# Whole loads of the branch inputs, eight sums moved to VectorE, and the second half of w_out loaded between evictions, in a hybrid pooling, convolution and attention block

## The chip, the cores and the metric

The kernel runs on one core of a Trainium2 chip. The metric is the device time of one execution in microseconds (us). Engines are named as in the profile: PE (TensorE, matrix products), PEld (its weight loads), DVE (VectorE), ACT (ScalarE), POOL (GpSimd), SP (SyncE, whose queue issues nearly all DMAs of this kernel).

## The reference

One layer over 1024 tokens of 1024 channels, in float32. A normed input is projected to ten groups of 512 columns and to 3 x 1024 merge-gate logits. Three branches (pooling, short convolution, stick-breaking attention) each give 512 channels, which are projected to 1024, weighted with a sigmoid gate and summed; an output projection and a norm follow.

```
def hybrid_layer(x, g_pre, w_in, pool_w, pool_scale, conv_w, conv_b, w_branch, w_out, g_post):
    h = rms_norm(x, g_pre)
    u = jnp.einsum('bsd,dn->bsn', h, w_in)
    (pool_v, pool_g, conv_x, conv_gb, conv_gc, conv_g,
     sb_q, sb_k, sb_v, sb_g, merge) = jnp.split(u, _split_points(), axis=-1)
    y_pool = pool_mixer(pool_v, pool_w, pool_scale) * jax.nn.silu(pool_g)
    y_conv = conv_mixer(conv_x, conv_gb, conv_gc, conv_w, conv_b) * jax.nn.silu(conv_g)
    y_sb = stick_breaking_attention(sb_q, sb_k, sb_v) * jax.nn.silu(sb_g)
    branches = jnp.stack([y_pool, y_conv, y_sb], axis=2)
    proj = jnp.einsum('bsnw,nwd->bsnd', branches, w_branch)
    gates = jax.nn.sigmoid(merge.reshape(b, s, N_BRANCH, D_MODEL))
    merged = jnp.sum(gates * proj, axis=2)
    out = jnp.einsum('bsd,de->bse', merged, w_out)
    return x + rms_norm(out, g_post)
```

## The kernel before

Activations lie with 128 channels on the partitions and the 1024 tokens along the free axis, in two halves of 512 (`HALVES`); blocks of 128 channels are numbered d = 0 to 7. Every product is made in three passes: both operands are split into a high and a low part (`split`: a cast to float32r on ACT for the high part, a subtraction on DVE or POOL for the low part), and low x high, high x low and high x high are accumulated in one PSUM bank of 128x512. So 12 products fill a bank of a half branch block, 24 one of the output projection.

The order of the work from the middle of the kernel on:

- **Gate pairs.** `gate_pair` makes two gate blocks of 128 channels from seven products of quarter blocks (`run_pair`, `product`). The products use three `g_ps` and two `q_ps` banks in turn. The results go into two tiles of tag `g` in the pool `gpool`, which has four such tiles of 128x1024; the pool also has two smaller tiles of tag `pr` (128x512).
- **First loop.** For the attention branch, four gate pairs multiply the projection that lies in DRAM (`proj_d`) by the gate and write it back (L695 to L700).
- **Pool branch.** `y_parts_of(yp_d)` loads the four blocks of the branch's output from DRAM in halves into the two `pr` tiles and splits them into `yhi` and `ylo` (pool `ypp`, four of each). `gated` then makes four pairs. After each pair, two branch blocks: `branch_proj` fills two `pp` banks of a pool of three (`ps_p`), 2 x 12 products, and `post` in `merged` multiplies by the gate (DVE, L716), adds the part so far, loaded from `proj_d` into `pr` tiles (POOL, L717), and writes the sum back (L722).
- **Conv branch.** The same with `y_parts_of(yc_d)`: two pairs with d = 0 to 3 in `gated`, then two pairs at once (`gs`, all four `g` tiles) and the **last four branch blocks**, d = 4 to 7, one after another. Their sums are not written back but split into the operands of the output projection (`take`, `take_merged`); `take` lags by one half. Meanwhile `taken_back` reads the sums of d = 0 to 3 back (`mr`) and splits them, and loads and splits the first half of w_out (`oh`).
- **Output projection.** The second half of w_out (`wo[1]`: load to one of three `wraw` tiles, cast on ACT, subtraction on POOL) is written in the code ahead of it. The tokens are worked in eight blocks of 128, first all with output columns 0 to 511, then all with 512 to 1023. Blocks 0 to 2 of the first half use the three `g` banks (`ahead`); from block 3 on `out_bank` alternates between `g` and `pp` banks. `first_half` squares a block's result with a row sum on ACT (L808) and scales it on DVE (L817), which frees the bank. In the second half the two variances are joined, and the result is scaled, added to x (`xr`, loaded into `g` tiles) and written out.

The order of the instructions on each engine is not that of the code alone: a planner arranges them when the program is built, by its own estimate of when each is ready, with earlier code first. On the chip every engine and SP's queue keep that order, and an instruction that waits holds what is behind it.

Of the kernel before, what the change touches and what calls it, by code (L numbers as in the profile page):

```python
# [8 lines left out]
F32 = mybir.dt.float32  # L9
F32R = mybir.dt.float32r  # L10
AF = mybir.ActivationFunctionType
ALU = mybir.AluOpType
PSUM = bass.MemoryType.PSUM

P = 128
D = 1024
S = 1024
KB = D // P
HALF = 512
# [7 lines left out]
HALVES = (slice(0, HALF), slice(HALF, S))  # L27
# [3 lines left out]
def f32(ap):  # L31
    return ap.bitcast(F32)
# [3 lines left out]
def hybrid_block_kernel(ctx, tc, x, g_pre, w_in, pool_w, pool_scale, conv_w, conv_b, w_branch, w_out, g_post, out):  # L36
# [12 lines left out]
    nc = tc.nc  # L49
    op = lambda name, bufs, **kw: ctx.enter_context(tc.tile_pool(name=name, bufs=bufs, **kw))  # L50

    const = op("const", 1)
    ps_g = op("ps_g", 3, space=PSUM)
# [18 lines left out]
    def split(raw, hi, lo, eng):  # L72
        nc.scalar.copy(hi, raw)  # L73
        eng.tensor_tensor(out=lo, in0=raw, in1=f32(hi), op=ALU.subtract)  # L74
# [29 lines left out]
    def next_w(ahead=2):  # L104
        while len(ready) < 1 + ahead:
            got = next(source, None)
            if got is None:
                break
            ready.append(got)
        return ready.pop(0)  # L110
# [210 lines left out]
    with tc.tile_pool(name="au", bufs=3) as au, \  # L321
# [106 lines left out]
        for n in range(len(steps) + LAG + 1):  # L428
            if n < len(steps):
                p, s, i = steps[n]  # L430
# [51 lines left out]
    def branch_proj(ys, weights, post, banks):  # L482
        whi, wlo = weights
        for t in range(2):
            pp = banks.tile([P, HALF], F32, tag="pp", name="pp")
            n = 0
            for k in range(NB):
                a = slice(k * P, (k + 1) * P)
                yh, yl = ys[k]
                for l, r in ((wlo, yh), (whi, yl), (whi, yh)):  # L490
                    nc.tensor.matmul(pp, l[:, a], r[:, HALVES[t]], start=(n == 0), stop=(n == 3 * NB - 1))  # L491
                    n += 1
            post(HALVES[t], pp)
# [49 lines left out]
    turn = [0]  # L543
# [133 lines left out]
    gpool = op("gates", 4, reuse_waits="tile")  # L677
# [6 lines left out]
    def part_of(src, ts):  # L684
        o = gpool.tile([P, HALF], F32, tag="pr", name="pr", bufs=2)
        nc.sync.dma_start(o, src[:, ts])
        return o

    def parts_in_dram(d):
        return [part_of(proj_d[d], ts) for ts in HALVES]  # L690
# [4 lines left out]
    for d in range(0, KB, 2):  # L695
        prs = parts_in_dram(d)
# [6 lines left out]
    def y_parts_of(srcs):  # L703
        parts = []
        for src in srcs:
            hi = ypp.tile([P, S], F32R, tag="yhi", name="yhi")
            lo = ypp.tile([P, S], F32R, tag="ylo", name="ylo")
            for ts in HALVES:
                split(part_of(src, ts), hi[:, ts], lo[:, ts], nc.vector)
            parts.append((hi, lo))  # L710
        return parts


    def merged(ys, d, g, prs, take):
        def post(ts, pp):
            nc.vector.tensor_tensor(out=g[:, ts], in0=pp, in1=g[:, ts], op=ALU.mult)  # L716
            nc.gpsimd.tensor_tensor(out=g[:, ts], in0=prs[0 if ts is HALVES[0] else 1], in1=g[:, ts], op=ALU.add)  # L717
            if take is not None:
                take(d, ts, g[:, ts])
        branch_proj(ys, next_w(), post, ps_p)  # L720
        if take is None:
            nc.sync.dma_start(proj_d[d], g)  # L722
# [16 lines left out]
    def out_weight(o, d, es):  # L739
        raw = wraw.tile([P, HALF], F32, tag="raw", name="wo_raw")  # L740
        nc.sync.dma_start(raw, w_out[d, :, es])
        split(raw, o[:, 0, :], o[:, 1, :], nc.gpsimd)
        return o[:, 0, :], o[:, 1, :]

    wo = ([], [])
# [16 lines left out]
    def take(*merged_half):  # L762

        waiting.append(merged_half)
        if len(waiting) > 1:
            take_merged(*waiting.pop(0))
        next(coming_back, None)

    gated(y_parts_of(yp_d))
    y_conv = y_parts_of(yc_d)  # L770
    gated(y_conv, 2)
    gs = gate_pair() + gate_pair()
# [10 lines left out]
    wo1p = op("wo1", KB, reuse_waits="tile")  # L783
    fin = held["m"]
    gpost_sb = fin.tile([P, D], F32, tag="gpost", name="gpost_sb")
    nc.sync.dma_start(gpost_sb, g_post.broadcast_to([P, D]))
    for d in range(KB):
        wo[1].append(out_weight(wo1p.tile([P, 2, HALF], F32R, tag="wo", name="wo"), d, HALVES[1]))


    def out_products(i, ps, ds, h, es):
        a = slice(i * P, (i + 1) * P)
        for d in ds:
            (mh, ml), (oh, ol) = m_parts[d], wo[h][d]
            for n, (l, r) in enumerate(((ml, oh), (mh, ol), (mh, oh))):
                nc.tensor.matmul(ps, l[:, a], r[:, es], start=(d == 0 and n == 0), stop=(d == KB - 1 and n == 2))  # L796

    turn = [0]

    def out_bank():  # L800
        turn[0] += 1
        return (ps_g.tile([P, HALF], F32, tag="g", name="o_ps") if turn[0] % 2
                else ps_p.tile([P, HALF], F32, tag="pp", name="o_ps"))

    def square(ps, var):
        junk = fin.tile([P, HALF], F32, tag="junk", name="junk")
        ssq = fin.tile([P, 1], F32, tag="ssq", name="ssq", bufs=4)
        nc.scalar.activation(junk[:, 0:ps.shape[-1]], ps, AF.Square, accum_out=ssq)  # L808
        o = fin.tile([P, 1], F32, tag="var", name="var", bufs=S // P + 4)
        if var is None:  # L810
            nc.vector.tensor_scalar(out=o, in0=ssq, scalar1=1.0 / D, scalar2=EPS, op0=ALU.mult, op1=ALU.add)
        else:
            nc.vector.scalar_tensor_tensor(out=o, in0=ssq, scalar=1.0 / D, in1=var, op0=ALU.mult, op1=ALU.add)
        return o

    def scaled(ps, o, es):
        nc.vector.tensor_tensor(out=o, in0=ps, in1=gpost_sb[:, es], op=ALU.mult)  # L817
# [3 lines left out]
    def first_half(i, ps):  # L821
        kept_var.append(square(ps, None))
        o = (held["raw"].tile([P, HALF], F32, tag="raw", name="o0") if i < 5
             else held["sum"].tile([P, HALF], F32, tag="s", name="o0"))
        scaled(ps, o, HALVES[0])
        kept_o.append(o)
# [6 lines left out]
    for i in range(n_tok):  # L833
        if i < 3:
            ps = ahead[i]
        else:
            ps = out_bank()
            out_products(i, ps, range(KB), 0, slice(0, HALF))
        first_half(i, ps)
    for i in range(n_tok):  # L840
        a = slice(i * P, (i + 1) * P)
        xr = gpool.tile([P, D], F32, tag="g", name="xr")
        nc.sync.dma_start(xr, x[a, :])
        o1 = gpool.tile([P, HALF], F32, tag="pr", name="o1", bufs=2)
        var = kept_var[i]
        pieces = (slice(0, HALF),) if i < n_tok - 1 else (slice(0, 256), slice(256, HALF))
        for es in pieces:
            ps = out_bank()[:, 0:es.stop - es.start]
            out_products(i, ps, range(KB), 1, es)
            var = square(ps, var)  # L850
            scaled(ps, o1[:, es], slice(HALF + es.start, HALF + es.stop))
        r = fin.tile([P, 1], F32, tag="rstd", name="rstd", bufs=2)
        nc.gpsimd.tensor_tensor(out=r, in0=var, in1=expo[:, 0:1], op=ALU.pow)
        for o, es in [(kept_o[i], HALVES[0])] + [(o1[:, es], slice(HALF + es.start, HALF + es.stop)) for es in pieces]:
            nc.vector.scalar_tensor_tensor(out=o, in0=o, scalar=r, in1=xr[:, es], op0=ALU.mult, op1=ALU.add)
            nc.sync.dma_start(out[a, es], o)
# [41 lines left out]
```

## Time and profile before

| | |
|---|---|
| median of 3 runs | 1049.41 us (1045.95 to 1049.87) |
| profiled execution | 1049.73 us, its span 1048.0 us |
| PE busy | 1004.6 us, 96% of the span |
| DVE, ACT, POOL busy | 625.9, 449.4, 460.1 us |
| mean granted TensorE clock | 0.988 |
| data moved | 97.09 MB, mean 93 GB/s |

The span is the time from the first to the last instruction on the core. In the list of waits a row reads: engine, tile and line of the instruction that waited, what it waited for, total, number of times, longest. In a timeline a row reads: start, length, engine, line, operation, output and inputs, count, and in brackets the engine's idle time before it with what ended it. A group's row gives the busy time and the mean of one in ns, then the idle time before them. For DMAs the time given is from the issue to the landing. A row of a tile gives minimum, median and maximum of an operation's length, and first and last start.

### The profile page before, as it was taken

The numbers are of one execution on the slowest core, as the hardware profiler recorded it, in microseconds if no ns is written. First come the engines' busy times: TensorE is split into PE (matmuls) and PEld (weight loads), VectorE is DVE, ScalarE is ACT, GpSimd is POOL, SyncE is SP. The second block draws the span as 40 slices with busy tenths as digits, with TensorE's granted clock in tenths as the row PEclk, the third lists the DMA queues.
The fourth block names the chain that finished last, engine by engine and source line by source line (L and its number), as shares of the span: only waits on it lengthen the run. The fifth ranks groups of instructions, "written<-read, shape, count | busy, mean of one in ns | idle before, by whom it ended". The sixth has DMA issues, their size and how long they took to land.

```text
span 1048.0 us, 13308 instructions
## 1 busy us (share of the span) xinstructions
PE 1004.6 (96%) x4752; PEld 829.0 (79%) x4752; DVE 625.9 (60%) x847; ACT 449.4 (43%) x879; POOL 460.1 (44%) x367
## 2 busy tenths in 40 slices
PE   4999999999998999999999999998999999998997
PEld 3788878888887888888888888886888888876886
DVE  6556777667777968798677675554333543342133
ACT  6567667567755543332222234333233332443111
POOL 3043544535472024455454444444555555576000
PEclk9999999999999999999999999998999999999999
DMA  6101000101011532122122134545333454164033
GB/s 229 53 21 41 22 21 21 41 21 32 21 31 41 191 131 71 61 70 91 61 81 61 61 111 144 190 136 173 118 120 124 161 171 131 34 221 157 1 121 121
DMA packets 45138, 97.09 MB, mean 93 GB/s; under 512 B 5392, under 2 KB 5648, under 8 KB 45072
## 3 DMA queue, kind: packets, MB, share of 16 engines
q1 hardware_dynamic: 44928, 95.71, 28.0%
q8 instruction: 38, 0.62, 0.2%
q10 hardware_dynamic: 144, 0.52, 0.1%
q14 instruction: 28, 0.23, 0.1%
HBM read 73.15 MB, written 23.07 MB: 92 GB/s over the span
## 4 chain that ended last, share of the span: by engine, by line
PE 82%; ACT 5%; DVE 4%; POOL 4%; issue 3%; DMA 2%; POOLq 0%; SPq 0%; DVEq 0%; ACTq 0%
PE g_ps L539 26%; PE q_ps L539 17%; PE g_ps L189 12%; PE pp L491 10%; PE o_ps L796 7%; PE o L418 3%; PE tp L404 2%; DVE sn L386 2%; PE z L382 1%; PE z L379 1%; ACT sn L383 1%; POOL sp L388 1%; POOL g L717 1%; DMA pr<-yp 1%; DMA xt<-in_x_dram 1%
## 5 line engine op out<-in xcount | busy, mean ns | idle before, releaser
L74 POOL TENSOR_TENSOR w_lo<-s,w_hi 128x512 fp32r<-128x512 f32 x95 | 130.7, 1376 | 173.8 <-ACT w_hi L73 171.2
L74 POOL TENSOR_TENSOR w_lo<-s_raw,w_hi 128x512 fp32r<-128x512 f32 x70 | 94.6, 1351 | 102.6 <-ACT w_hi L73 96.8
L388 POOL TENSOR_TENSOR sp<-sp,sn 128x127 f32<-128x127 f32 (+3 forms) x64 | 81.2, 1272 | 132.8 <-DVE sn L386 69.0
L386 DVE TENSOR_TENSOR_SCAN sn<-sn,zeros 128x128 f32<-128x128 f32 (+3 forms) x64 | 100.6, 1574 | 48.2 <-ACT sn L383 45.5
L73 ACT CAST w_hi<-s 128x512 fp32r<-128x512 f32 x96 | 59.6, 621 | 134.1 <-PE g_ps L539 65.7
L73 ACT CAST w_hi<-s_raw 128x512 fp32r<-128x512 f32 x70 | 43.5, 621 | 138.2 <-PE g_ps L539 53.8
L189 PE MATMUL g_ps<-hh,w_hi 128*128 128x512 f32 x240 | 99.4, 414 | 0.3 <-ACT hh L285 0.3
L189 PE MATMUL g_ps<-hl,w_hi 128*128 128x512 f32 x240 | 94.5, 394 | 0.3 <-DVE hl L286 0.3
L189 PE MATMUL g_ps<-hh,w_lo 128*128 128x512 f32 x240 | 94.5, 394 | 0.0
L74 POOL TENSOR_TENSOR w_lo<-w_raw,w_hi 128x512 fp32r<-128x512 f32 x44 | 68.2, 1550 | 56.3 <-ACT w_hi L73 56.3
L539 PE MATMUL g_ps<-hh,w_hi 128*128 128x512 f32 x236 | 92.6, 392 | 0.0
L539 PE MATMUL g_ps<-hh,w_lo 128*128 128x512 f32 x236 | 92.1, 390 | 0.0
L539 PE MATMUL g_ps<-hl,w_hi 128*128 128x512 f32 x236 | 91.8, 389 | 0.0
L491 PE MATMUL pp<-yhi,w_lo 128*128 128x512 f32 x192 | 77.1, 402 | 5.0 <-ACT yhi L73 2.6
L491 PE MATMUL pp<-ylo,w_hi 128*128 128x512 f32 x192 | 76.8, 401 | 0.9 <-DVE ylo L74 0.9
L491 PE MATMUL pp<-yhi,w_hi 128*128 128x512 f32 x192 | 76.4, 399 | 0.0
L383 ACT ACTIVATE sn<-z 128x384 f32<-128x384 f32 (+2 forms) x96 | 47.9, 499 | 29.7 <-PE z L382 20.3
L232 DVE TENSOR_TENSOR wl<-tp,wh 128x512 fp32r<-128x512 f32 (+2 forms) x96 | 50.4, 545 | 15.4 <-ACT wh L405 14.9
L539 PE MATMUL q_ps<-hh,w_hi 128*128 128x512 f32 x148 | 58.1, 392 | 0.0
L539 PE MATMUL q_ps<-hh,w_lo 128*128 128x512 f32 x148 | 57.8, 391 | 0.0
L539 PE MATMUL q_ps<-hl,w_hi 128*128 128x512 f32 x148 | 57.5, 389 | 0.0
L405 ACT CAST wh<-tp 128x512 fp32r<-128x512 f32 (+2 forms) x96 | 44.6, 493 | 21.8 <-PE tp L404 17.2
(204 smaller groups left out, 2426.4 us busy)
## 6 DMA issues: line engine op xcount, KB each, us to landing
s_raw<-in_w_in_dram SPq DMA_DIRECT2D x96, 256.0 KB, 2.6
pr<-proj SPq DMA_DIRECT2D x48, 256.0 KB, 3.3
proj<-g SPq DMA_DIRECT2D x20, 512.0 KB, 2.9
w_raw<-in_w_in_dram SPq DMA_DIRECT2D x34, 256.0 KB, 2.6
w_raw<-in_w_branch_dram SPq DMA_DIRECT2D x24, 256.0 KB, 2.6
xt<-in_x_dram SPq DMA_DIRECT2D x8, 512.0 KB, 7.9
proj<-proj SPq DMA_DIRECT2D x8, 512.0 KB, 2.7
wo_raw<-in_w_out_dram SPq DMA_DIRECT2D x16, 256.0 KB, 2.9
```

What stands on the lines that cost most here:

```text
L73: nc.scalar.copy(hi, raw)
L74: eng.tensor_tensor(out=lo, in0=raw, in1=f32(hi), op=ALU.subtract)
L189: nc.tensor.matmul(ps, l[:, a], r[k // 4][t][:, k % 4, :], start=(n == 0), stop=(n == 3 * KB - 1))
L232: nc.vector.tensor_tensor(out=o, in0=a, in1=f32(b), op=ALU.subtract)
L383: nc.scalar.activation(sn[:, c0:c1], z[:, :w], AF.Sigmoid, scale=-0.125)
L386: nc.vector.tensor_tensor_scan(out=rev, data0=rev, data1=zeros.to_broadcast([P, n]), initial=1.0, op0=ALU.mult, op1=ALU.max)
L388: nc.gpsimd.tensor_tensor(out=sp[:, 0:n - 1], in0=sp[:, 0:n - 1], in1=sn[:, 1:n], op=ALU.mult)
L405: nc.scalar.copy(wh[c][:, 0:m, qsub], tp[:, 0:m, :])
L418: nc.tensor.matmul(o[:, cs], vc[:, j, s, :], wt[j // 4][:, j % 4, cs], start=(j == 0 and wt is wl), stop=(j == i and wt is wh))
L491: nc.tensor.matmul(pp, l[:, a], r[:, HALVES[t]], start=(n == 0), stop=(n == 3 * NB - 1))
L539: nc.tensor.matmul(bank, l[:, a], r[:, j, :], start=(n == 0), stop=(n == 11))
L796: nc.tensor.matmul(ps, l[:, a], r[:, es], start=(d == 0 and n == 0), stop=(d == KB - 1 and n == 2))
```

## The change

Three edits. (1) `y_parts_of` loads each block of a branch's output whole, 128x1024 in one DMA, into a tile of tag `g`, and splits it with one cast and one subtraction; the `pr` tiles are no longer used for it. (2) In `merged`, where `take` is given (the last four branch blocks), the sum of L717 is made by DVE in place of POOL; elsewhere it stays on POOL. (3) The loads and splits of the second half of w_out move from ahead of the output projection into its first loop, one behind each `first_half`; and `out_bank` gives a `pp` bank for its first three calls (blocks 3, 4 and 5) and then a `g` bank on even turns, a `pp` bank on odd ones.

```
--- before.py
+++ after.py
@@ -705,8 +705,9 @@
         for src in srcs:
             hi = ypp.tile([P, S], F32R, tag="yhi", name="yhi")
             lo = ypp.tile([P, S], F32R, tag="ylo", name="ylo")
-            for ts in HALVES:
-                split(part_of(src, ts), hi[:, ts], lo[:, ts], nc.vector)
+            y = gpool.tile([P, S], F32, tag="g", name="y")
+            nc.sync.dma_start(y, src)
+            split(y, hi, lo, nc.vector)
             parts.append((hi, lo))
         return parts
 
@@ -714,7 +715,8 @@
     def merged(ys, d, g, prs, take):
         def post(ts, pp):
             nc.vector.tensor_tensor(out=g[:, ts], in0=pp, in1=g[:, ts], op=ALU.mult)
-            nc.gpsimd.tensor_tensor(out=g[:, ts], in0=prs[0 if ts is HALVES[0] else 1], in1=g[:, ts], op=ALU.add)
+            adder = nc.gpsimd if take is None else nc.vector
+            adder.tensor_tensor(out=g[:, ts], in0=prs[0 if ts is HALVES[0] else 1], in1=g[:, ts], op=ALU.add)
             if take is not None:
                 take(d, ts, g[:, ts])
         branch_proj(ys, next_w(), post, ps_p)
@@ -784,8 +786,6 @@
     fin = held["m"]
     gpost_sb = fin.tile([P, D], F32, tag="gpost", name="gpost_sb")
     nc.sync.dma_start(gpost_sb, g_post.broadcast_to([P, D]))
-    for d in range(KB):
-        wo[1].append(out_weight(wo1p.tile([P, 2, HALF], F32R, tag="wo", name="wo"), d, HALVES[1]))
 
 
     def out_products(i, ps, ds, h, es):
@@ -799,7 +799,7 @@
 
     def out_bank():
         turn[0] += 1
-        return (ps_g.tile([P, HALF], F32, tag="g", name="o_ps") if turn[0] % 2
+        return (ps_g.tile([P, HALF], F32, tag="g", name="o_ps") if turn[0] > 3 and turn[0] % 2 == 0
                 else ps_p.tile([P, HALF], F32, tag="pp", name="o_ps"))
 
     def square(ps, var):
@@ -837,6 +837,7 @@
             ps = out_bank()
             out_products(i, ps, range(KB), 0, slice(0, HALF))
         first_half(i, ps)
+        wo[1].append(out_weight(wo1p.tile([P, 2, HALF], F32R, tag="wo", name="wo"), i, HALVES[1]))
     for i in range(n_tok):
         a = slice(i * P, (i + 1) * P)
         xr = gpool.tile([P, D], F32, tag="g", name="xr")
```

More of the change, by code (lines that the diff above doesn't have):

```diff
@@ L707, in y_parts_of @@
             lo = ypp.tile([P, S], F32R, tag="ylo", name="ylo")
-            for ts in HALVES:
-                split(part_of(src, ts), hi[:, ts], lo[:, ts], nc.vector)
+            y = gpool.tile([P, S], F32, tag="g", name="y")
+            nc.sync.dma_start(y, src)
+            split(y, hi, lo, nc.vector)
             parts.append((hi, lo))
@@ L716, in post @@
             nc.vector.tensor_tensor(out=g[:, ts], in0=pp, in1=g[:, ts], op=ALU.mult)
-            nc.gpsimd.tensor_tensor(out=g[:, ts], in0=prs[0 if ts is HALVES[0] else 1], in1=g[:, ts], op=ALU.add)
+            adder = nc.gpsimd if take is None else nc.vector
+            adder.tensor_tensor(out=g[:, ts], in0=prs[0 if ts is HALVES[0] else 1], in1=g[:, ts], op=ALU.add)
             if take is not None:
@@ L786, in hybrid_block_kernel @@
     nc.sync.dma_start(gpost_sb, g_post.broadcast_to([P, D]))
-    for d in range(KB):
-        wo[1].append(out_weight(wo1p.tile([P, 2, HALF], F32R, tag="wo", name="wo"), d, HALVES[1]))
     def out_products(i, ps, ds, h, es):
@@ L801, in out_bank @@
         turn[0] += 1
-        return (ps_g.tile([P, HALF], F32, tag="g", name="o_ps") if turn[0] % 2
+        return (ps_g.tile([P, HALF], F32, tag="g", name="o_ps") if turn[0] > 3 and turn[0] % 2 == 0
                 else ps_p.tile([P, HALF], F32, tag="pp", name="o_ps"))
@@ L839, in hybrid_block_kernel @@
         first_half(i, ps)
+        wo[1].append(out_weight(wo1p.tile([P, 2, HALF], F32R, tag="wo", name="wo"), i, HALVES[1]))
     for i in range(n_tok):
```

## The prediction

> **What bounds the kernel.** I read the page's top first, then the list of TensorE's own waits, then windows over the stages of the change.
>
> ```profile
> span 1048.0 us, 13308 instructions
> PE 1004.6 (96%) x4752; PEld 829.0 (79%) x4752; DVE 625.9 (60%) x847; ACT 449.4 (43%) x879; POOL 460.1 (44%) x367
> ```
>
> TensorE is busy 96% of the span, and the change takes no product away. What it can win is idle TensorE time and time at a reduced clock, nothing else. So the list of waits comes next (total, times, longest); these four rows are the ones in the part that the change touches:
>
> ```profile
> PE o_ps L796 <- DVE o L817: 4.7, 1, 4.7
> PE pp L491 <- ACT yhi L73: 2.6, 2, 1.4
> PE pp L491 <- DVE g L716: 2.4, 2, 2.1
> PE pp L491 <- DVE ylo L74: 0.9, 1, 0.9
> ```
>
> Each edit has its wait: the staging of the pool branch's y (2.6 + 0.9), the last four branch blocks (2.4), the start of the output projection (4.7). A wait costs more than its own length, which the windows show; PEclk is the granted clock.
>
> ```profile
> core 0: us, PE busy (x) PEld busy (x) DVE busy (x) ACT busy (x) POOL busy (x), PEclk, DMA share, GB/s
> 711.72:729.54 17.82, 14.32 (x50) 10.53 (x49) 7.79 (x11) 5.82 (x10) 7.67 (x6) 0.81 0.50 170
> 749.06:759.94 10.88, 10.88 (x49) 9.01 (x49) 2.77 (x4) 1.74 (x3) 6.42 (x5) 1.00 0.35 117
> 919.48:945.82 26.34, 23.93 (x98) 19.03 (x96) 12.09 (x16) 10.76 (x18) 18.61 (x13) 0.94 0.67 221
> 945.82:1041.80 95.98, 91.07 (x409) 74.70 (x407) 25.88 (x52) 17.53 (x45) 20.38 (x20) 0.96 0.29 96
> ```
>
> The second row is the yardstick: two branch blocks (48 products) without a wait take 10.88. The first row is the same work behind the staging: 17.82 at a mean clock of 0.81, so **6.94 lost**, 3.5 by waiting and about 0.19 x 17.82 = 3.4 by the clock. The third holds the last four blocks: 26.34 against 2 x 10.88 = 21.76, **4.58 lost**, 2.4 by waiting and 0.06 x 26.34 = 1.6 by the clock. The fourth, the output projection, comes below.
>
> **Part by part. 1, whole loads into gate tiles (L705 to L709).** Now:
>
> ```profile
> 686.79 2.38 SPq L129 DMA_DIRECT2D s_raw<-in_w_in_dram  x2
> 687.63 0.68 DVE L585 TENSOR_TENSOR g<-q_ps,u 128x512 f32<-128x512 f32 x1
> 694.89 1.06 SPq L700 DMA_DIRECT2D proj<-g  x2
> 696.00 1.76 SPq L686 DMA_DIRECT2D pr<-yp  x2
> 697.80 7.94 SPq L129 DMA_DIRECT2D s_raw<-in_w_in_dram  x2
> 715.92 1.62 SPq L686 DMA_DIRECT2D pr<-yp  x2
> 702.86 0.62 ACT L73 CAST yhi<-pr 128x512 fp32r<-128x512 f32 x1 [4.39 <-DMA pr<-yp]
> proj<-g SPq DMA_DIRECT2D x20, 512.0 KB, 2.9
> mr<-proj SPq DMA_DIRECT2D x4, 512.0 KB, 4.7
> DMA to landing us min/median/max: 2.6/3.6/6.8
> L74 DVE TENSOR_TENSOR m<-mr,m 128x1024 fp32r<-128x1024 f32 x4 | 5.5, 1386 | 2.6 <-ACT m L73 2.6
> L73 ACT CAST m<-mr 128x1024 fp32r<-128x1024 f32 x4 | 4.2, 1046 | 0.6 <-DMA mr<-proj 0.6
> 885.22 0.32 SPq L722 DMA_DIRECT2D proj<-g  x1
> 936.37 0.38 SPq L843 DMA_DIRECT2D xr<-in_x_dram  x1
> ```
>
> Eight half loads go two by two through the two pr tiles, which the proj loads hold until 696; the last pair starts at 715.92, four microseconds after TensorE is ready for it (711.72). After the change four loads of 512 KB use the four gate tiles. Gate tiles seem to be handed out in the order of the code: one pair's write-back at 885.22 freed two, yet the later xr loads, which need only such a tile, begin at 936.37. So y0 and y1 wait until the pair before has its second tile, first written at 687.63, and then take the two tiles of the pair before that, long written back. Put behind the two s_raw loads that SP issues there (686.79 to 689.2), they start near 689 and land by 694 (4.7 for a 512 KB read), 2 us before the first half load is even issued now. y2 and y3 take the tiles whose write-back is issued at 694.89 (landing after 2.9) or those of y0 and y1 after their split: issued near 698.5, landed between 703 and, with the slowest landing of a yp load (6.8, the row of minimum, median and maximum), 706. One cast and one subtraction of 128x1024 each (1.05 and 1.39, the m<-mr rows) put the last operand at about 708.5. TensorE needs y0 at 711.7 and y3, its tenth to twelfth product there, 9 x 10.88 / 48 = 2.0 later, at 713.7. Slack: 5 us. In the worst placement, y2 and y3 stand on SP behind the s_raw pair that holds the queue from 697.80 for 7.94: issued at 705.8, landed at 710.5 to 712.6, ready at 713 to 715. That is a wait of 0 to 1.5; with a little more on DVE, 2. **Take -6.94**; bounds 0 (the loads are as late as now) and -6.94.
>
> The first gate tile of the next pair is handed out behind y3. It is wanted near 701 and a tile is free from about 698.5. Should it be late, TensorE still has the five banks that products use in turn. Eight DMA issues leave SP; DVE and ACT process the same elements in half as many instructions. The conv branch's y is staged the same way at 820 to 840, under a pair of gates, where the list shows no wait of TensorE before and I expect none after: 0. What is next in line behind the y parts is the first branch weight; its cast stands on ACT behind the y casts and comes forward with them.
>
> **2, sums by VectorE (L717).** Eight additions leave POOL for DVE.
>
> ```profile
> 937.22 0.68 DVE L716 TENSOR_TENSOR g<-pp,g 128x512 f32<-128x512 f32 x1
> 942.20 0.68 DVE L716 TENSOR_TENSOR g<-pp,g 128x512 f32<-128x512 f32 x1
> 934.64 1.29 POOL L717 TENSOR_TENSOR g<-pr,g 128x512 f32<-128x512 f32 x1
> 935.96 0.62 ACT L73 CAST m<-g 128x512 fp32r<-128x512 f32 x1 [4.04 <-POOL g L717]
> L717 POOL TENSOR_TENSOR g<-pr,g 128x512 f32<-128x512 f32 x8 | 10.3, 1286 | 4.1 <-DVE g L716 4.1
> L716 DVE TENSOR_TENSOR g<-pp,g 128x512 f32<-128x512 f32 x8 | 5.5, 684 | 0.8 <-PE pp L491 0.8
> L74 DVE TENSOR_TENSOR m<-g,m 128x512 fp32r<-128x512 f32 x8 | 6.4, 805 | 20.0 <-ACT m L73 20.0
> L699 DVE TENSOR_TENSOR g<-g,pr 128x512 f32<-128x512 f32 x16 | 14.4, 903 | 8.5 <-ACT g L594 8.4
> L133 DVE TENSOR_TENSOR s<-s_raw x14: 691/693/1776, 697.8 to 893.9; 128x512 f32<-128x512 f32 x14
> ```
>
> The chain of one half is product, DVE multiplication, POOL addition, ACT cast, DVE subtraction. The subtraction stands on DVE ahead of a later multiplication, so the multiplication, which frees the pp bank, waits for POOL: the fourth (937.22) and the fifth (942.20) lie 5.0 apart, where the list has TensorE wait for them. POOL has 10.3 of additions here between weight splits. On DVE one addition costs between 0.69 and 1.78 (the ends of L133, same shapes and also two SBUF inputs); I take 0.90, the mean of L699, which reads the same tiles. A half is then 0.68 + 0.90 + 0.81 = 2.39, under the 2.72 that TensorE takes for it (10.88 / 4). From the first multiplication near 922.2, with two of the four mr subtractions (2.8) still to do, the fifth starts by 922.2 + 4 x 2.39 + 2.8 = 934.6 and ends at 935.3. The eighth half, which needs that bank, starts at 919.48 + 7 x 2.72 = 938.5: 3.2 in hand. With 1.78 each it would be 0.3 late. The pr load of the half after next also starts earlier. **Take -4.58**; bounds -4.58 and 0.
>
> The Trainium skill, "SBUF — State Buffer", section "Who interferes with whom", speaks against this edit: a DVE instruction with two SBUF inputs and a GpSimd instruction reading SBUF exclude each other, the later one waiting the whole instruction. The L133 maximum agrees: 0.69 plus nearly a POOL operation of 1.29 is near 1.78. By it, if every addition met a POOL operation, the sum would lose the 0.3 above and no more.
>
> **3, second half of w_out and other banks (L787, L802).**
>
> ```profile
> 953.21 1.66 ACT L73 CAST wo<-wo_raw 128x512 fp32r<-128x512 f32 x3
> 964.92 1.32 ACT L73 CAST wo<-wo_raw 128x512 fp32r<-128x512 f32 x2 [1.29 <-DMA wo_raw<-in_w_out_dram]
> 966.14 0.59 ACT L808 ACTIVATE junk<-o_ps 128x512 f32<-128x512 f32 x1
> 980.76 0.60 ACT L808 ACTIVATE junk<-o_ps 128x512 f32<-128x512 f32 x1 [4.39 <-issue]
> 986.28 0.60 ACT L808 ACTIVATE junk<-o_ps 128x512 f32<-128x512 f32 x1 [4.83 <-issue]
> 997.07 44.48 PE L796 MATMUL o_ps<-wo,m 128*128 128x512 f32 x216
> ```
>
> Eight wo casts, 953.21 to 966.1, stand on ACT ahead of the first square (966.14), and token block 3 wants the bank that this square and its DVE partner free. Undisturbed, a token block takes 5.52 (986.28 - 980.76), so the first half is 8 x 5.52 = 44.16; the second takes 44.48; together 88.64. TensorE ran from 945.82 to 997.07 + 44.48 = 1041.55, 95.73: **7.09 lost**, 4.7 waiting and the rest clock. Afterwards blocks 3, 4 and 5 go to the three pp banks, free since the last branch block, so the first bank is wanted again after six blocks (33 us), not three. That alone covers the late square. The moved loads keep their eight DMAs on SP, eight casts and eight POOL splits. Even if ACT kept every wo behind its block's square, the last one, cast after block 7, is split 0.8 + 0.6 + 1.3 later, while its product is 21 products of 0.23 (5.52 / 24) = 4.8 into the second half; with its load (as long as one of 512 KB, 2.9) behind as well it would be 0.8 late, and such a gap could bring the half clock (1.6, as in the third window). **Take -7.09**; bounds -7.09 and -4.6.
>
> **Sum.** 1049.73 (the profiled execution; span 1048.0) - 6.94 - 4.58 - 7.09 = 1031.12. The median of the runs, 1049.41, is 0.3 lower, so the sum serves for both; I say 1031.
>
> **Rivals.** (a) The staging wait survives in part: the worst placement of part 1, 2 us of wait. The third window shows that one gap of 2.1 brought the half clock, so another 1.6 (its clock loss above) to 3.4: 1035 to 1036.5. For: SP is a single queue and was held 7.94 there. Against: 5 us of slack otherwise. The Trainium skill, "TensorE: Matmul & The Clock Gate", section "Why this matters for your kernels", advises only against gaps over about 3 us; by it this rival costs 2, but the 0.94 clock behind a 2.1 gap decides otherwise.
> (b) DVE becomes the limit of the last four blocks, by contention with POOL or an addition waiting for its pr load with the multiplication queued behind: up to all 4.58 back, 1035.7. For: DVE work is 2.39 of each 2.72. Against: three banks of lead.
> (c) Slower: the new loads and additions give another order on the engines in the seven gate pairs between 730 and 919, so that weights miss their product there. Place: each pair's first product; price: a wait of 2.1 and 1.6 of clock, 3.7 per pair as in the third window. Five pairs (18.5) eat the gain, and it is slower than before by more than a measurement tells from the seventh: 25.9 - 18.6 = 7.3 over, 1057. Against: TensorE has no wait there now, and those lines stay.
> (d) No change: the y loads get no tile before 698 and go two by two as now, and DVE is the limit too; only part 3 is left, and a block of weights late by 0.8 with two half-clock windows takes 3.4 of it: 1046.
>
> **How the numbers follow.** Forecast 0.70, (a) 0.12, (b) 0.10, (c) 0.03, (d) 0.05. A measurement of this kernel tells about 0.5% (5 us) from no change. Faster: forecast, (a) and (b), 0.92; same 0.05; slower 0.03. The range goes from 1027 (the lowest run before lay 3.5 under the median, so a run may come out that much lower) to 1038 (a or b, or a little of both).
>
> **What would show it.** Right: no TensorE wait on yhi, ylo, g L716 or o L817 in the list; 48 products after 711.7 in about 10.9; four last blocks in 21.8; output projection 88.6; clock 1.00 in all three; yp loads issued near 689 and 698. Wrong: a wait on yhi from a load after 705; DVE additions above 1.5 with a wait on g L716; squares or second-half products waiting on wo; any new wait between 730 and 919.

## The result, and the profile after

The changed kernel takes **1032.44 us** (median of 4 runs, 1032.07 to 1033.10) against 1048.99 us before (4 runs, 1045.95 to 1049.87), a ratio of **0.9837** (95% interval 0.9818 to 0.9856). The forecast was 1031, range 1027 to 1038. The profiled execution took 1032.51.

The top of the page after, and the whole list of TensorE's waits from 600 us on (total, times, longest). Lines from L709 on have moved by two at most: the multiplication of `merged` is now L717, its sum L719.

```profile
span 1030.7 us, 13275 instructions
PE 997.1 (97%) x4752; PEld 825.0 (80%) x4752; DVE 636.5 (62%) x847; ACT 447.8 (43%) x871; POOL 453.0 (44%) x359
```

```profile
PE pp L491 <- DVE g L717: 0.7, 1, 0.7
```

Of the four rows of before one is left, and it is short. The same stages as windows (columns as in the prediction; the granted clock is the third number from the end):

```profile
711.81:722.69 10.88, 10.88 (x49) 9.01 (x48) 2.97 (x5) 2.98 (x6) 7.67 (x6) 1.00 0.48 154
912.99:935.77 22.78, 22.10 (x97) 17.95 (x96) 19.09 (x22) 10.82 (x18) 12.93 (x8) 1.00 0.76 250
935.77:1024.41 88.64, 88.64 (x409) 73.16 (x407) 28.26 (x54) 17.33 (x43) 16.98 (x17) 1.00 0.31 105
```

The two blocks behind the staging take 10.88, the yardstick exactly: 6.94 won. The last four blocks take 22.78: 3.56 won, with 1.02 over the yardstick's 21.76. The output projection takes 88.64, the number worked out for it undisturbed: 7.09 won. The three make 17.59 (6.94 + 3.56 + 7.09); the two profiled executions differ by 17.22, and the 0.4 between these numbers is less than the 1.0 by which the runs after differ among themselves.

The timelines of the staging after, SP's queue, then rows of DVE and ACT, show how near the y parts came to their computed times:

```profile
687.32 0.90 SPq L709 DMA_DIRECT2D y<-yp  x2
693.52 2.71 SPq L709 DMA_DIRECT2D y<-yp  x2
696.51 2.02 SPq L700 DMA_DIRECT2D proj<-g  x2
692.27 1.23 DVE L74 TENSOR_TENSOR ylo<-y,yhi 128x1024 fp32r<-128x1024 f32 x1
694.66 1.23 DVE L74 TENSOR_TENSOR ylo<-y,yhi 128x1024 fp32r<-128x1024 f32 x1 [0.56 <-ACT yhi L73]
701.18 1.05 ACT L73 CAST yhi<-y 128x1024 fp32r<-128x1024 f32 x1 [2.04 <-DMA y<-yp]
702.87 2.34 DVE L74 TENSOR_TENSOR ylo<-y,yhi 128x1024 fp32r<-128x1024 f32 x1
```

Two loads go out at 687.3, about when the pair before first writes its second tile (687.79); the other two are issued from 693.52 on, right behind the end of y0's subtraction (692.27 + 1.23 = 693.50) and before the write-backs are issued (696.51), so they took the tiles of y0 and y1. Two gate tiles thus carried all four loads, where the prediction spoke of four. The last subtraction ends at 705.2, where 708.5 was forecast, 8.5 us before its first use.

### The profile page after: what moved, and what is told of

Same layout as the page of the kernel before. It is cut to its first block, busy times and chain, and to the rows that moved or that the text cites. A ratio compares the mean times of both kernels' runs of the same rounds, so it can differ in the third digit from the quotient of the medians.

```text
span 1030.7 us, 13275 instructions
## 1 busy us (share of the span) xinstructions
PE 997.1 (97%) x4752; PEld 825.0 (80%) x4752; DVE 636.5 (62%) x847; ACT 447.8 (43%) x871; POOL 453.0 (44%) x359
## 4 chain that ended last, share of the span: by engine, by line
PE 84%; ACT 5%; DVE 4%; POOL 3%; issue 2%; DMA 2%; SPq 0%; POOLq 0%; DVEq 0%; ACTq 0%
PE g_ps L539 26%; PE q_ps L539 17%; PE g_ps L189 12%; PE pp L491 11%; PE o_ps L796 8%; PE o L418 3%; PE tp L404 2%; DVE sn L386 2%; PE z L382 1%; PE z L379 1%; POOL w_lo L74 1%; POOL sp L388 1%; ACT sn L383 1%; DMA xt<-in_x_dram 1%; ACT sp L384 1%
## 5 line engine op out<-in xcount | busy, mean ns | idle before, releaser
L491 PE MATMUL pp<-yhi,w_lo 128*128 128x512 f32 x192 | 75.0, 392 | 0.7 <-DVE g L717 0.7
L383 ACT ACTIVATE sn<-z 128x384 f32<-128x384 f32 (+2 forms) x96 | 47.9, 499 | 29.7 <-PE z L382 20.4
L133 DVE TENSOR_TENSOR s<-s_raw 128x512 f32<-128x512 f32 x48 | 41.9, 873 | 23.4 <-POOL w_lo L74 22.8
```

What stands on the lines that cost most here:

```text
L133: nc.vector.tensor_tensor(out=o, in0=a, in1=b, op=how)
L383: nc.scalar.activation(sn[:, c0:c1], z[:, :w], AF.Sigmoid, scale=-0.125)
```

## The experiments

Each ratio is to the kernel before on the same chip; its medians were 1049.27 beside the first four experiments, 1048.46 beside the next four and 1048.96 beside the last two. "Over the changed kernel" is counted from 1032.44; the third experiment, whose queues turned out to be the changed kernel's, gives 1032.26 beside the first four.

**Four kernels that each take one part back.** First the halves through the pr tiles:

```
-            y = gpool.tile([P, S], F32, tag="g", name="y")
-            nc.sync.dma_start(y, src)
-            split(y, hi, lo, nc.vector)
+            for ts in HALVES:
+                split(part_of(src, ts), hi[:, ts], lo[:, ts], nc.vector)
```

> The changed kernel with the y parts loaded in halves through the two pr tiles again; sums on VectorE, w_out and banks as changed. Theory A (three separate waits that add up): the staging wait and its half clock return, 6.9 us: 1039.4, with TensorE waits on yhi/ylo of about 3.5 in total and nothing else new. Rival B (the whole loads gained by something shared with the other edits, so that the parts do not add): less than 4, 1036 or below.

Measured: 1036.98 (1036.55 to 1037.81), ratio 0.9885 (0.9869 to 0.9902), 4.5 over the changed kernel. The waits are the expected ones, in the list of TensorE's waits, beside the 0.7 that the changed kernel has too:

```profile
PE pp L491 <- ACT yhi L73: 2.2, 2, 1.2
PE pp L491 <- DVE ylo L74: 0.9, 1, 0.9
```

Mechanism as in A, size between A and B. The waits (3.1 in place of 3.5) are nearly as long as before; the clock loss is half as large: see the last section.

Second, the sums on POOL again:

```
-            adder = nc.gpsimd if take is None else nc.vector
-            adder.tensor_tensor(...)
+            nc.gpsimd.tensor_tensor(...)
```

> The changed kernel with the sums of the last four branch blocks on GpSimd again. Theory A: the wait on the branch multiplications returns (26.3 in place of 22.8 for the four blocks), 3.6 us: 1036, while the output projection stays free of waits, since blocks 3 to 5 have other banks. Rival B (VectorE's sums bring the whole chain of the projection forward, and the banks alone do not cover it): TensorE also waits on o L817 or on wo, 1039 or more.

Measured: 1036.90 (1036.07 to 1037.84), 0.9885 (0.9867 to 0.9902), 4.5 over. TensorE waits on the multiplication alone; the projection has no wait, so A:

```profile
PE pp L491 <- DVE g L717: 4.0, 2, 2.1
```

The wait is longer than before the change (2.4): the four blocks take 27.7, where A had 26.3.

Third, the second half of w_out written ahead of the projection again:

```
     nc.sync.dma_start(gpost_sb, g_post.broadcast_to([P, D]))
+    for d in range(KB): wo[1].append(out_weight(wo1p.tile(...), d, HALVES[1]))
...
-        wo[1].append(out_weight(wo1p.tile(...), i, HALVES[1]))
```

> The changed kernel with the second half of w_out written ahead of the output projection again. Theory A (placing it in the code changes nothing, because the planner issues these loads and splits as soon as they are ready, ahead of every square in both): same time as the changed kernel, 1032.4, and the wo casts on ScalarE still all ahead of the first square. Rival B (splitting it between the evictions is what freed the first banks): a TensorE wait on o L817, 1035 to 1039.

Measured: 1032.26 (1031.94 to 1033.75), 0.9843 (0.9826 to 0.9860). A holds, and more plainly than expected: in the two traces every engine runs the same instructions in the same order. ACT's timeline in the changed kernel shows why; here are the first three and the last two of the eight casts of w_out, and the first square:

```profile
940.24 1.85 ACT L73 CAST wo<-wo_raw 128x512 fp32r<-128x512 f32 x3
950.81 1.34 ACT L73 CAST wo<-wo_raw 128x512 fp32r<-128x512 f32 x2 [1.29 <-DMA wo_raw<-in_w_out_dram]
952.05 0.59 ACT L808 ACTIVATE junk<-o_ps 128x512 f32<-128x512 f32 x1
```

All eight casts still stand ahead of the first square. The code says "between evictions", the queue does not.

Fourth, the old alternation of banks:

```
-        ... if turn[0] > 3 and turn[0] % 2 == 0
+        ... if turn[0] % 2
```

> The changed kernel with the output banks alternating from the first call again (block 3 takes a bank of blocks 0 to 2). Theory A (as forecast: the other banks carry the whole 7.1 of the output projection): 1039.5, TensorE waiting 4.7 on o L817. Rival B (the sums on VectorE end the branch blocks' chain earlier, so the first square is only about 1 us late and the banks cover little): a wait of about 1.4 and at most 1.7 of clock, 1034 to 1035.5.

Measured: 1033.88 (1033.42 to 1034.40), 0.9856 (0.9839 to 0.9872), 1.4 over. B: the wait on the bank is back, but it is short, and it brings no clock loss (from 930 to 975 the granted clock is 1.00).

```profile
PE o_ps L796 <- DVE o L817: 1.3, 1, 1.3
PE pp L491 <- DVE g L717: 0.7, 1, 0.7
```

**Three kernels that make one part alone** on the kernel before. The whole loads:

> The kernel before with only the whole y loads into gate tiles. Theory A (the staging wait stands alone): 6.9 less, 1042; TensorE still waits on g L716 and o L817 as before. Rival B (time won here is lost again at a later wait): under 3 less.

Measured: 1043.78 (1043.01 to 1044.62), 0.9954 (0.9937 to 0.9970), 4.7 less. No wait at the staging; both later waits stay, that of the projection slightly longer (5.1 against 4.7):

```profile
PE o_ps L797 <- DVE o L818: 5.1, 1, 5.1
PE pp L491 <- DVE g L717: 2.4, 2, 2.1
```

A by its waits, short of A's 6.9 in size; the last section shows that the clock loss of the staging wait differs from profile to profile.

The sums:

> The kernel before with only the sums of the last four branch blocks on VectorE. Theory A (the sums free the chain behind them too: the wo casts, and with them the first square, come earlier, so the wait on o L817 shrinks from 4.7 to about 1.4): 3.6 for the blocks and 4 to 5.7 in the output projection, 1040 to 1042. Rival B (the two waits are independent): 3.6 less, 1045.5, with the 4.7 on o L817 still there.

Measured: 1040.28 (1040.03 to 1041.35), 0.9921 (0.9905 to 0.9937), 8.2 less: A.

```profile
PE pp L491 <- ACT yhi L73: 2.5, 2, 1.3
PE o_ps L797 <- DVE o L818: 1.4, 1, 1.4
PE pp L491 <- DVE ylo L74: 0.9, 1, 0.9
PE pp L491 <- DVE g L716: 0.7, 1, 0.7
```

The sums shorten not only the wait of the blocks (2.4 to 0.7) but also that of the projection (4.7 to 1.4): the blocks' results no longer come late through POOL, so the wo casts behind them on ACT, and then the first square, come earlier. Counted from the projection's first product, the first square starts after 20.3 before the change (966.14 - 945.82) and after 17.1 here (product at 943.00):

```profile
960.11 0.59 ACT L809 ACTIVATE junk<-o_ps 128x512 f32<-128x512 f32 x1
```

The banks:

> The kernel before with only the other banks for blocks 3 to 5. Theory A: the banks alone cover the late square, the wait on o L817 goes with its half clock, 7.1 less: 1042. Rival B (the wait moves to a later block or to the second half of w_out): under 4 less, with a new TensorE wait in the output projection.

Measured: 1041.67 (1040.47 to 1043.67), 0.9936 (0.9918 to 0.9954), 6.8 less: A. There is no wait in the projection, though the first square is late: ACT's timeline in that kernel has it behind the last two casts at

```profile
964.51 0.59 ACT L808 ACTIVATE junk<-o_ps 128x512 f32<-128x512 f32 x1
```

which is 20.4 after the projection's first product (944.08). Block 3 is due after 16.6 (3 x 5.52), and TensorE worked on in three other banks.

So each of two parts alone takes away most of the projection's wait. Alone they win 4.7 + 8.2 + 6.8 = 19.7, together 16.55: the sums and the banks overlap.

**What in the whole loads helps.** The changed kernel, each part in a gate tile but loaded and split in two halves:

```
-            nc.sync.dma_start(y, src)
-            split(y, hi, lo, nc.vector)
+            for ts in HALVES:
+                nc.sync.dma_start(y[:, ts], src[:, ts])
+                split(y[:, ts], hi[:, ts], lo[:, ts], nc.vector)
```

> The changed kernel with each y part still in a gate tile of its own, but loaded and split in two halves (eight loads of 256 KB, eight casts, eight subtractions). Theory A (the gain is that four tiles are free early): as the changed kernel, 1032.4, no TensorE wait on yhi or ylo. Rival B (the gain is the larger load and fewer instructions): part of the staging wait returns, 1034 to 1039.

Measured: 1032.32 (1031.79 to 1032.79), 0.9844 (0.9826 to 0.9861): the changed kernel's time, with no wait on yhi or ylo. A in time and waits: the size of a load and the number of instructions do not count. What remains is the gate tiles, and of these, as the timeline above shows, two and not four: they are free at 687, where the pr tiles are held until 696, and each takes in two halves at a time. No run separates the earlier start from the double room.

**Two tries at the 0.7 that is left.** Sums of second halves on POOL (`adder = nc.gpsimd if take is None or ts is HALVES[1] else nc.vector`):

> The changed kernel, but of the last four branch blocks only the first half's sum is on VectorE, the second half's on GpSimd. Theory A (what is left there is VectorE's own pace: multiplication, sum, a wait for the cast, subtraction, 3.1 a half against TensorE's 2.7): with four sums fewer VectorE keeps up, the 0.7 wait on the multiplication goes, about 1 less, 1031.3. Rival B (GpSimd is still too late behind its weight splits, and VectorE stands behind its sum as before): a wait of 1 to 2 on the multiplication, with its half clock 1034 to 1036.

Measured: 1032.32 (1032.19 to 1032.40), 0.9838 (0.9820 to 0.9855). Neither: the wait is still 0.7. VectorE's groups in 913 to 946 (operation, count, busy time, mean in ns, idle time before them) show where its time went:

```profile
L74 DVE TENSOR_TENSOR m<-g,m 128x512 fp32r<-128x512 f32 x8 | 8.4, 1056 | 8.5 <-ACT m L73 8.3
L719 DVE TENSOR_TENSOR g<-pr,g 128x512 f32<-128x512 f32 x4 | 4.9, 1230 | 0.1
```

Four sums fewer, but 8.3 us idle ahead of the subtractions (4.1 in the changed kernel), because half of the casts now wait for POOL, and subtractions of 1.06 in place of 0.88 on the mean.

Subtractions of second halves on POOL (in `take_merged`, the last argument `nc.vector if d < 4 or ts is HALVES[0] else nc.gpsimd`):

> The changed kernel, all eight sums on VectorE, but the subtraction that splits the second half of each of the last four blocks on GpSimd. Theory A (VectorE no longer stands idle for the cast in front of these four subtractions, and does four operations fewer): the 0.7 wait goes, about 1 less, 1031.3. Rival B (the extra GpSimd work and its exclusion with VectorE's two-input operations take it back): same as the changed kernel, 1032.4, or up to 2 more.

Measured: 1031.57 (1031.31 to 1032.39), 0.9833 (0.9816 to 0.9851). In its profile TensorE waits for nothing from 600 us on. That is theory A; the gain of 0.9 in the medians lies within the scatter of single runs, so it is shown by the list of waits rather than by the time. It is the fastest version of this study, if by a margin that the times alone do not prove.

## Why the prediction was right, point by point

**Bound.** Right. TensorE's work stayed, and the win is its idle time and clock: the windows after account for the difference within 0.4.

**Part 1** (-6.94): right, with the profile measuring 6.94. The order of the loads was as worked out. They came earlier than reckoned: y0 and y1 by 1.7 (687.3 for 689), y2 and y3 by 5.0 (693.5 for 698.5), the last operand by 3.3 (705.2 for 708.5). y2 and y3 took the tiles of y0 and y1, one of the two ways named, so that "four loads of 512 KB use the four gate tiles" did not hold. That whole loads as such do nothing was not in the prediction.

**Part 2** (-4.58 taken, -3.56 measured): the mechanism held, the step "A half is then 0.68 + 0.90 + 0.81 = 2.39" was mis-sized. VectorE's groups of the changed kernel in 913 to 946:

```profile
L719 DVE TENSOR_TENSOR g<-pr,g 128x512 f32<-128x512 f32 x8 | 9.2, 1154 | 0.2
L74 DVE TENSOR_TENSOR m<-g,m 128x512 fp32r<-128x512 f32 x8 | 7.0, 876 | 4.2 <-ACT m L73 4.1
L717 DVE TENSOR_TENSOR g<-pp,g 128x512 f32<-128x512 f32 x8 | 5.5, 682 | 0.8 <-PE pp L491 0.8
```

A sum costs 1.15, not 0.90, and VectorE stands idle for 4.1 in all in front of the subtractions, about 0.5 a half: 0.68 + 1.15 + 0.88 + 0.51 = 3.2 a half, over TensorE's 2.72. I had left the idle time out, because the code lets the subtraction lag one half. The timeline shows that the planner put it right behind its own sum and cast:

```profile
928.71 1.80 DVE L719 TENSOR_TENSOR g<-pr,g 128x512 f32<-128x512 f32 x1
931.20 1.02 DVE L74 TENSOR_TENSOR m<-g,m 128x512 fp32r<-128x512 f32 x1 [0.69 <-ACT m L73]
932.14 0.68 DVE L717 TENSOR_TENSOR g<-pp,g 128x512 f32<-128x512 f32 x1
932.85 0.69 DVE L719 TENSOR_TENSOR g<-pr,g 128x512 f32<-128x512 f32 x1
```

The fifth multiplication ends at 932.8, 19.8 us after the blocks' start (912.99), where 15.8 was forecast (935.3 against 919.48); the eighth half could have begun at 19.04 (7 x 2.72). Hence the 0.7 wait. It is part of rival (b), at a small price, and one of the prediction's signs of being wrong came with it: two of the eight sums took over 1.5 (1.78 and 1.80). Of the 1.02 that the four blocks lost, the wait is 0.68; the other 0.34 is time in which TensorE was busy (22.10 for 21.76), and its cause stays open.

Between the first multiplication (915.91) and the fifth (932.14) both terms count about equally: the four sums take 5.7 in place of 3.6 (4 x 0.90), and VectorE stands idle for 2.0. The last two experiments change both terms at once, so they do not tell them apart. With four sums on POOL the same stretch takes 16.3, as in the changed kernel (16.2): what the sums no longer take comes back as idle time and longer subtractions. With four subtractions on POOL it takes 14.2: two of them lie in the stretch, 1.9 less work, and the idle time is 0.6 shorter.

As for the rule of the Trainium skill ("SBUF — State Buffer", "Who interferes with whom") that a VectorE operation with two SBUF inputs and a reading GpSimd operation exclude each other: the eight sums of the changed kernel agree with it one by one. The three that no POOL operation overlaps take 0.68 or 0.69, the five that overlap one take 1.08 to 1.80. The sum at 928.71 (1.80) meets this pair of POOL operations, the sum at 932.85 (0.69) comes after it:

```profile
928.67 3.00 POOL L74 TENSOR_TENSOR oh<-wo_raw,oh 128x512 fp32r<-128x512 f32 x2 [2.40 <-ACT oh L73]
```

The mean sum rises to 1.40 where four more POOL operations stand in that stretch, in the kernel with subtractions of second halves on POOL:

```profile
L719 DVE TENSOR_TENSOR g<-pr,g 128x512 f32<-128x512 f32 x8 | 11.2, 1404 | 1.8 <-DMA pr<-proj 1.7
```

No run takes POOL's work away from that stretch, so that it is the cause rests on this overlap and is not shown by an experiment. The prediction's price for it, 0.3 with every sum at 1.78, was too low because the idle time was missing from the sum to which it was added.

**Part 3** (-7.09): the size was right, and so was "that alone covers the late square" (only the banks: no wait). But of the two edits only the banks do anything; the move in the code changed no queue. And in the changed kernel the banks are worth 1.4, because part 2 had already brought the first square forward. So the 7.09 was right as the loss of that place, not as the worth of that edit. The sum came out right because it was made from the places where time was lost, each counted once, not from what each edit is worth alone.

**Rivals.** (a), (c) and (d) did not come: no wait on yhi or ylo, none between 730 and 912, and the loads found tiles at 687.

## What to carry to other kernels

Where one engine is busy 96% of the span, add up its waits with their clock loss by place, against an undisturbed stretch of the same work: that gives the sum of several edits, while their single gains may overlap (here 19.7 alone, 16.55 together). A wait on a load can be a wait for a free tile: two larger tiles that were free earlier took it away, and the size of the loads did not matter. When instructions are ordered by a planner, look in the timeline at what stands in front of what; a lag or a placement written in the code may not be there.

## What the runs showed of the hardware

The clock loss behind a wait is not fixed by the wait's length; what else decides it stays open. The staging waits (3.1 to 4.3 in several pieces within 8 us) went with a mean clock of 0.74, 0.87 and 1.00 over the 13 us from 711 to 724; these rows (start, end, length, TensorE busy, granted clock, DMA share, GB/s) are of the sums alone, of the halves through the pr tiles and of the banks alone:

```profile
711.00:724.00 13.00, 9.59 (x30) 0.74 0.51 164
```

```profile
711.00:724.00 13.00, 9.95 (x35) 0.87 0.56 181
```

```profile
711.00:724.00 13.00, 8.68 (x36) 1.00 0.56 182
```

That is 3.4, 1.7 and 0 us of lost clock (0.26, 0.13 and 0 of 13 us), in steps of 1.7; the longest waits, 4.3 with a piece of 2.4, are those without loss. This fits the 4.5 that the halves through the pr tiles cost, against the 6.9 that one execution of the kernel before showed. It may also be why that kernel's runs (1046.25 to 1051.24 beside the second group of experiments) scatter more than the changed one's (1.0); no run was made to test it. From 900 us on, single waits of 0.7 to 1.4 brought no loss in any profile taken here: over the 45 us from 930 to 975 the clock is 1.00 in the kernel with the sums alone, which has waits of 0.65 and 1.44 there, and 0.96 where the banks alone left a wait of 2.08:

```profile
930.00:975.00 45.00, 42.91 (x186) 1.00 0.47 147
```

```profile
930.00:975.00 45.00, 42.59 (x178) 0.96 0.44 141
```

A single wait of 2.1 thus sufficed, in that kernel, in the kernel before and in that with the whole loads alone. It does not always: in the changed kernel with the sums on POOL the first wait, of 2.09, left the clock at 1.00, and the loss came behind the second, of 1.96:

```profile
931.17 0.47 PE L491 MATMUL pp<-yhi,w_lo 128*128 128x512 f32 x1 [2.09 <-DVE g L717]
936.10 0.50 PE L491 MATMUL pp<-yhi,w_lo 128*128 128x512 f32 x1 [1.96 <-DVE g L717]
928.00:936.00 8.00, 4.05 (x17) 1.00 0.64 197
936.00:944.00 8.00, 7.90 (x27) 0.79 0.58 183
```

The advice of the Trainium skill ("TensorE: Matmul & The Clock Gate", "Why this matters for your kernels") against idle gaps over about 3 us is too lenient for this kernel.
